# Two-operand elementwise work from GpSimd to VectorE, first expert loads before the gather, LN2's first results in PSUM

## The chip, the cores and the metric

The kernel runs on one core of one Trainium2 chip, in one launch. The metric is device time in microseconds, the median of the runs shown; smaller is better. Five engines take part, each with a queue of its own: TensorE (PE, with its weight loads as PEld), VectorE (DVE), ScalarE (ACT), GpSimd (POOL), and SyncE (SP), which issues most DMAs.

## The reference

A sequence of 256 tokens with 1024 features goes through two blocks, all in float32. The first block is two hybrid layers and a norm; the second is one mixer with four branches, LayerNorm (LN1), a mixture of experts and LayerNorm again (LN2). Cut to what matters:

```
# hybrid_layer, twice
h = rms_norm(x, norm_mix_g) * (1 + sc_m) + sh_m
proj = h @ w_in
...
merged = (jax.nn.sigmoid(ga) * (o_na @ w_br_na)
          + jax.nn.sigmoid(gb) * (o_mla @ w_br_mla)
          + jax.nn.sigmoid(gc) * (o_gqa @ w_br_gqa))
x = x + g_m * (merged @ w_out)
h = rms_norm(x, norm_ffn_g) * (1 + sc_f) + sh_f
gate, up = jnp.split(h @ ffn_w_gate_up, 2, axis=-1)
x = x + g_f * ((jax.nn.silu(gate) * up) @ ffn_w_down)
# second_block
h = mixer(x, ...)
x = layer_norm(DN_ALPHA * x + h, ln1_g[l], ln1_b[l])
h = moe(x, w_router, router_bias, w_gate[l], w_up[l], w_down[l])
x = layer_norm(DN_ALPHA * x + h, ln2_g[l], ln2_b[l])
```

Each token goes to 2 of 16 experts. The kernel collects each expert's tokens by matrix products with a selection matrix P (the gather); an expert is two 1024x512 products, an activation, and one 512x1024 product.

## The kernel before

**Matrix products in three.** Every float32 matrix is split into a high part (rounded to fp32r) and a low remainder, and a product is three matmuls: high x high (line 189), and the two mixed ones (190 and 191). For weights, `raw` lets SP load up to 1 MB (128 x 2048, line 152) into a ring of buffers (`wr`); `pieces` makes each half of it, 128 x 1024, into two parts: ACT casts the high part (`wh`, line 159), and DVE subtracts (`wl`, line 164), or POOL does (line 162). The rings `wh` and `wl` have five buffers each. For activations, ACT casts (231, 276, 306) and DVE subtracts (232, 277, 307).

**Who subtracts.** `s.hold` is a list that `pieces` takes one entry from: POOL, or an instruction behind which the subtraction must stand, or nothing. `norm_end` fills it with three entries of POOL from the table `HOLD`, so the first three weight pieces loaded after it are subtracted by POOL. `moe` fills it for the first expert: two pieces by DVE, two by POOL, two by DVE behind the building of P.

```
a = s.hold.pop(0) if s.hold else None
if a is s.nc.gpsimd:
    a.tensor_sub(lo, src, hi)
```

**Other POOL work with two operands.** The squares that a norm sums up over four pairs of feature blocks: POOL adds the second and third, DVE the fourth (`norm_add`, 288). The gated sum of the three branches, two adds for each of four column blocks and each layer (816, 16 in all). The mask of the neighbourhood attention (695, 8), the last add of the rotary step (538, 6), the gated merge of the mixer's branches (1544, 8), one quarter of LN1's second token half (1716 and 1717, behind an ACT step at 1715), the low parts of LN1's output (1728 and 1827), and the last quarter of LN2 (1983 and 1984). POOL also issues DMAs: the modulation weights (400), the attention bias (690) and constants.

**Order.** The program is written in stage order, and a scheduler then orders each engine's queue by the data that each instruction needs; a queue is worked off in its order. So the place of an instruction in a queue isn't always that of the code. Names in the rows begin with a stage: `L_lat`, `L_gqaqkv` and others are the head of a layer (its projections), `L_branch` and `L_wout` the end of its attention, `L_gu` and `L_down` its FFN; `M_` is the mixer (`M_rg` and `M_gdn` its first branches, `M_out` its output projection, `M_ln` LN1), `E_` the experts.

**LN1 to the gather** (`out_norm`, `route`, `moe`). The output projection is computed in eight tiles; behind the tiles of a token half stand the statistics, the normalised rows `x2` (`norm_apply`, two DVE steps of 128 x 256 for each quarter, 1642 and 1643), the router's score, the selection, the slot numbers `pos`, the matrix P (1841), then the gather's products (1852), which ACT and DVE copy out of PSUM (1855, 1857). The gather is a generator: it yields after each product.

**The end** (`out_rows`). LN2's sums stand in four PSUM banks of 128 x 512, `z`. For three of them `norm_apply` reads PSUM and writes to SBUF (1642), then reads that and writes the output rows (1643); the fourth goes over ACT and POOL. Each is stored by its own DMA (1987).

## Time and profile before

| | |
|---|---|
| runs | 1613.37 us median of 3 (1607.16 to 1614.84) |
| the profiled execution | 1609.31 us, of which the profile's span is 1607.5 |
| PE, DVE, ACT, POOL busy in the span | 96%, 75%, 56%, 14% |
| granted clock of PE, mean over the span | 0.985 of full speed |
| DMA, mean over the span | 215 GB/s |

The profile is of one execution, whose own time is in the second line. Busy shares are over the whole span; where an engine waits, the view of waits names the engine and line that it waited for, and the timeline lists instructions with start, duration and, in brackets, the idle time before one. A duration in the timeline that carries x2 or x4 is of that many instructions in a row together.

### The profile page before, as it was taken

To read this page: it belongs to the slowest core of one execution; us is meant where nothing else is said; L and a number is where in the kernel's file an instruction comes from. 1 tells how busy PE (TensorE), PEld (TensorE's weight loads), DVE (VectorE), ACT (ScalarE), POOL (GpSimd) and SP (SyncE) were. 2 spreads that over 40 slices of the span, in tenths; PEclk is the share of its full clock that TensorE was granted. 3 is DMA by queue.
4 is the path that set the end of the run, shared out by engine and by line. 5 is a ranking of instruction groups with operands and counts; after the bars stand their busy time and mean duration, and the time that the engine had idled before them with its cause. 6 is when DMAs were issued, how large, how long until landed. Compare 5 with 4: busy or idle time off the path is not lost.

```text
span 1607.5 us, 28047 instructions
## 1 busy us (share of the span) xinstructions
PE 1541.4 (96%) x11376; PEld 1419.1 (88%) x11376; DVE 1208.0 (75%) x1615; ACT 900.9 (56%) x1316; POOL 218.7 (14%) x236
## 2 busy tenths in 40 slices
PE   7899999999999999899998999999999899999996
PEld 5789999999987989899998989999999778888884
DVE  5889778767597886784547976567666788988886
ACT  4555546444465554544445771665565377777774
POOL 0221033102032102400002004112020110000000
PEclk9999999999999999999999999999999899999998
DMA  9678547886556864665553650334556489999982
GB/s 349 220 251 282 165 151 256 293 281 213 169 170 215 285 208 139 212 233 184 184 186 124 185 158 27 106 105 138 179 180 213 139 321 333 333 325 334 340 324 94
DMA packets 206055, 345.77 MB, mean 215 GB/s; under 512 B 6928, under 2 KB 175008, under 8 KB 193632
## 3 DMA queue, kind: packets, MB, share of 16 engines
q1 hardware_dynamic: 191040, 294.42, 54.9%
q0 software_dynamic: 12512, 45.64, 7.9%
q10 hardware_dynamic: 2368, 3.86, 0.7%
q8 instruction: 91, 1.49, 0.4%
q14 instruction: 44, 0.36, 0.1%
HBM read 342.84 MB, written 1.05 MB: 214 GB/s over the span
## 4 chain that ended last, share of the span: by engine, by line
PE 85%; DVE 8%; ACT 3%; POOL 2%; issue 1%; DMA 1%; DVEq 0%; POOLq 0%; ACTq 0%
PE L_gu.mm L190 5%; PE L_gu.mm L191 4%; PE L_gu.mm L189 4%; PE L_att.mm L189 3%; PE L_att.mm L191 3%; PE L_att.mm L190 3%; PE M_merge.mm L191 2%; PE M_merge.mm L189 2%; PE M_merge.mm L190 2%; PE E_gu.mm L189 2%; PE E_gu.mm L191 2%; PE E_gu.mm L190 2%; PE L_gu.s L190 1%; PE L_gu.s L189 1%; PE L_gu.s L191 1%; PE L_att.s L424 1%
## 5 line engine op out<-in xcount | busy, mean ns | idle before, releaser
L190 PE MATMUL L_gu.mm<-L_fnorm.hl,L_gu.wh 128*128 128x256 f32 x640 | 178.9, 280 | 0.2
L191 PE MATMUL L_gu.mm<-L_fnorm.hh,L_gu.wl 128*128 128x256 f32 x640 | 178.9, 280 | 0.0
L189 PE MATMUL L_gu.mm<-L_fnorm.hh,L_gu.wh 128*128 128x256 f32 x640 | 178.6, 280 | 0.1
L164 DVE TENSOR_TENSOR E_gu.wl<-E_gu.wr,E_gu.wh 128x1024 fp32r<-128x1024 f32 x126 | 153.7, 1241 | 19.6 <-ACT E_gu.wh L159 16.3
L159 ACT CAST L_gu.wh<-L_gu.wr 128x1024 fp32r<-128x1024 f32 x84 | 88.2, 1050 | 119.7 <-PE L_gu.mm L190 79.2
L159 ACT CAST E_gu.wh<-E_gu.wr 128x1024 fp32r<-128x1024 f32 x128 | 132.8, 1054 | 36.7 <-PE E_gu.mm L191 10.2
L164 DVE TENSOR_TENSOR L_gu.wl<-L_gu.wr,L_gu.wh 128x1024 fp32r<-128x1024 f32 x78 | 96.3, 1238 | 66.3 <-ACT L_gu.wh L159 66.1
L189 PEld LDWEIGHTS L_gu.mm<-L_fnorm.hh,L_gu.wh 128*128 128x128 f32 x640 | 120.2, 188 | 0.5 <-ACT L_fnorm.hh L306 0.5
L190 PEld LDWEIGHTS L_gu.mm<-L_fnorm.hl,L_gu.wh 128*128 128x128 f32 x640 | 120.1, 188 | 0.6 <-DVE L_fnorm.hl L307 0.6
L191 PEld LDWEIGHTS L_gu.mm<-L_fnorm.hh,L_gu.wl 128*128 128x128 f32 x640 | 120.3, 188 | 0.0
L159 ACT CAST L_down.wh<-L_down.wr 128x1024 fp32r<-128x1024 f32 x48 | 50.5, 1051 | 77.0 <-PE L_gu.mm L190 42.9
L393 DVE SCALAR_TENSOR_TENSOR ada.big<-ada.big,sc,ada.big 128x1024 f32<-128x1024 f32 x70 | 92.3, 1318 | 0.2
L164 DVE TENSOR_TENSOR L_down.wl<-L_down.wr,L_down.wh 128x1024 fp32r<-128x1024 f32 x48 | 59.8, 1246 | 40.2 <-ACT L_down.wh L159 40.1
L164 DVE TENSOR_TENSOR E_down.wl<-E_down.wr,E_down.wh 128x1024 fp32r<-128x1024 f32 x64 | 75.5, 1222 | 4.3 <-ACT E_down.wh L159 4.2
L159 ACT CAST L_att.wh<-L_att.wr 128x1024 fp32r<-128x1024 f32 x44 | 46.2, 1051 | 55.4 <-PE L_att.mm L190 48.3
L400 POOL DMA_DIRECT2D ada.big<-in_ada_w x80 | 42.4, 532 | 251.4 <-DVE ada.big L393 160.4
L164 DVE TENSOR_TENSOR M_merge.wl<-M_merge.wr,M_merge.wh 128x1024 fp32r<-128x1024 f32 (+1 forms) x50 | 55.2, 1109 | 27.8 <-ACT M_merge.wh L159 27.8
L159 ACT CAST E_down.wh<-E_down.wr 128x1024 fp32r<-128x1024 f32 x64 | 65.8, 1057 | 13.0 <-PE E_down.mm L191 4.5
L159 ACT CAST M_merge.wh<-M_merge.wr 128x1024 fp32r<-128x1024 f32 (+1 forms) x50 | 41.9, 843 | 43.8 <-PE M_merge.mm L190 40.2
L191 PE MATMUL M_merge.mm<-fnorm.hh,M_merge.wl 128*128 128x256 f32 x208 | 59.1, 284 | 0.0
L189 PE MATMUL M_merge.mm<-fnorm.hh,M_merge.wh 128*128 128x256 f32 x208 | 58.0, 279 | 0.0
L190 PE MATMUL M_merge.mm<-fnorm.hl,M_merge.wh 128*128 128x256 f32 x208 | 57.8, 278 | 0.0
(972 smaller groups left out, 5552.5 us busy)
## 6 DMA issues: line engine op xcount, KB each, us to landing
...
```

Source lines behind the costliest of these rows:

```text
L159: s.nc.scalar.copy(hi, src)
L164: i = s.nc.vector.tensor_sub(lo, src, hi).ins
L189: mm(ps, ah, bh, start=first and fresh and k == 0, stop=False, skip_group_check=True)
L190: mm(ps, ah, bl, start=False, stop=False, skip_group_check=True)
L191: mm(ps, al, bh, start=False, stop=last and k == n - 1, skip_group_check=True)
L393: nc.vector.scalar_tensor_tensor(acc, raw, c, acc, op0=ALU.mult, op1=ALU.add)
L400: s.tc.keep_in_program_order(nc.gpsimd.dma_start(raw, s.I["ada_w"][l, k * 128:(k + 1) * 128, v * 1024:(v + 1) * 1024]))
L424: nc.tensor.matmul(S[e][:, b], q[e][:, b * 128:(b + 1) * 128], k[e], start=True, stop=True)
```

## The change

All of the two-operand work named above except LN2's last quarter goes from POOL to DVE, and the table `HOLD` goes. LN1's quarter goes through `norm_apply` like the others. The low part of LN1's first token half stands behind the next tile in the code, that of the second half behind the building of P. The first expert's gate weights are loaded and cast ahead of the gather (`early`): the first load with its subtractions, the second with its subtractions collected in `s.defer` and issued after the gather's steps. The first gather takes all high parts before the low parts. LN2's first step writes its result back into PSUM, and the second step reads it from there.

```diff
@@ -17,7 +17,6 @@
 NB = 6
-HOLD = [3, 3, 3, 3]
@@ -109,6 +108,7 @@
         s.more, s.nraw = None, 0
+        s.defer = None
@@ -158,12 +158,12 @@
         a = s.hold.pop(0) if s.hold else None
-        if a is s.nc.gpsimd:
-            a.tensor_sub(lo, src, hi)
-        else:
-            i = s.nc.vector.tensor_sub(lo, src, hi).ins
-            if a:
-                s.after(i, a)
+        if s.defer is not None:
+            s.defer.append(lambda: s.nc.vector.tensor_sub(lo, src, hi))
+            return hi, lo
+        i = s.nc.vector.tensor_sub(lo, src, hi).ins
+        if a:
+            s.after(i, a)
@@ -285,11 +285,9 @@
         else:
-            (nc.vector if i == 3 else nc.gpsimd).tensor_add(s.zq, s.zq, q)
+            nc.vector.tensor_add(s.zq, s.zq, q)
...
     def norm_end(s, **k):
-        s.hold = [s.nc.gpsimd] * HOLD[0]
-        HOLD.append(HOLD.pop(0))
@@ -535,7 +533,7 @@
         nc.vector.scalar_tensor_tensor(qn[:, :nj], qn[:, :nj], f, bc(C["cg"]), op0=ALU.mult, op1=ALU.mult)
-        nc.gpsimd.tensor_add(qg[:, 2 * i:2 * i + nj], qn[:, :nj], sb[:, :nj])
+        nc.vector.tensor_add(qg[:, 2 * i:2 * i + nj], qn[:, :nj], sb[:, :nj])
@@ -692,7 +690,7 @@
                 bv = b.rearrange("p (d c) -> p d c", c=64)
-                nc.gpsimd.tensor_tensor(bv, bv, C["mask"].unsqueeze(1).to_broadcast([128, 8, 64]), ALU.add)
+                nc.vector.tensor_tensor(bv, bv, C["mask"].unsqueeze(1).to_broadcast([128, 8, 64]), ALU.add)
@@ -813,7 +811,7 @@
                     t2 = s.t([128, 512], "b2", NB)
-                    nc.gpsimd.tensor_add(t2, m, t)
+                    nc.vector.tensor_add(t2, m, t)
@@ -1541,7 +1539,7 @@
             if not first:
-                (nc.vector if out else nc.gpsimd).tensor_add(mi, mi, t)
+                nc.vector.tensor_add(mi, mi, t)
@@ -1710,13 +1708,7 @@
                         c = slice(q * 256, (q + 1) * 256)
-                        if b and q == 3:
-                            v = x2[:, b, c]
-                            nc.scalar.activation(v, ax[b][:, c], AF.Identity, bias=mr[:, b:b + 1], scale=r[:, b:b + 1])
-                            nc.gpsimd.tensor_mul(v, v, g[:, c])
-                            nc.gpsimd.tensor_add(v, v, bb[:, c])
-                        else:
-                            s.norm_apply(x2, ax[b][:, c], mv, r, g, bb, b, c)
+                        s.norm_apply(x2, ax[b][:, c], mv, r, g, bb, b, c)
@@ -1725,7 +1717,8 @@
                 nc.scalar.copy(xh[:, 0], x2[:, 0])
-                nc.gpsimd.tensor_sub(xl[:, 0], x2[:, 0], xh[:, 0])
+            if (i, b) == (2, 1):
+                nc.vector.tensor_sub(xl[:, 0], x2[:, 0], xh[:, 0])
@@ -1824,7 +1817,6 @@
         s.after(nc.scalar.copy(xh[:, 1], x2[:, 1]).ins, s.load_ins)
-        nc.gpsimd.tensor_sub(xl[:, 1], x2[:, 1], xh[:, 1])
@@ -1840,22 +1832,24 @@
                                             s.C3["iota"].unsqueeze(1).to_broadcast([128, 2, SLOTS]), ALU.is_equal).ins
+            G[g] = P, gh, gl
+            todo = [(k, src, dst) for k in range(0, 8, 2) for src, dst in ((xh, gh), (xl, gl))]
             if g == 0:
-                s.hold = [None, None, nc.gpsimd, nc.gpsimd, i, i]
-            G[g] = P, gh, gl
-            for k in range(0, 8, 2):
-                for src, dst in ((xh, gh), (xl, gl)):
-                    LAB[0] = 'E_gather.'
-                    p = bank()
-                    for i in range(2):
-                        for b in range(2):
-                            nc.tensor.matmul(p[:, i * 256:(i + 1) * 256], src[:, b, (k + i) * 128:(k + i + 1) * 128], P[:, b], start=b == 0, stop=b == 1)
-                    d = f(dst[:, k:k + 2])
-                    if src is xh:
-                        nc.scalar.copy(d, p)
-                    else:
-                        nc.vector.tensor_copy(d, p)
-                    yield
+                s.after(nc.vector.tensor_sub(xl[:, 1], x2[:, 1], xh[:, 1]).ins, i)
+                todo = todo[::2] + todo[1::2]
+                yield
+            for k, src, dst in todo:
+                LAB[0] = 'E_gather.'
+                p = bank()
+                for i in range(2):
+                    for b in range(2):
+                        nc.tensor.matmul(p[:, i * 256:(i + 1) * 256], src[:, b, (k + i) * 128:(k + i + 1) * 128], P[:, b], start=b == 0, stop=b == 1)
+                d = f(dst[:, k:k + 2])
+                if src is xh:
+                    nc.scalar.copy(d, p)
+                else:
+                    nc.vector.tensor_copy(d, p)
+                yield
@@ -1875,13 +1869,15 @@
+        early = []
+
...
             for c in range(2):
-                w = s.load_mov(I[W][e, c], 4, 512)
+                w = early.pop(0) if early else s.load_mov(I[W][e, c], 4, 512)
@@ -1918,9 +1914,13 @@
         G = {}
-        s.more = s.a
+        early.append(s.load_mov(I["wg"][0, 0], 4, 512))
...
         next(steps)
+        s.defer = []
+        early.append(s.load_mov(I["wg"][0, 1], 4, 512))
+        later, s.defer = s.defer, None
+        s.more = s.a
@@ -1933,6 +1933,8 @@
             pass
+        for sub in later:
+            sub()
@@ -1977,13 +1979,15 @@
                 c = slice(d * 512, d * 512 + 512)
+                v = o[:, b, c]
                 if b * d:
-                    v = o[:, b, c]
...
                 else:
-                    s.norm_apply(o, z[b][d], mv, r, g, bb, b, c)
+
+                    nc.vector.scalar_tensor_tensor(z[b][d], z[b][d], mv[:, b, 0:1], g[:, c], op0=ALU.subtract, op1=ALU.mult)
+                    nc.vector.scalar_tensor_tensor(v, z[b][d], r[:, b:b + 1], bb[:, c], op0=ALU.mult, op1=ALU.add)
```

Line numbers of the changed kernel differ by a few from those before. The order of DVE's queue is shown at three places, from the built programs. First, ahead of the FFN of layer 0; `L_wout.hl` is the low part of the scaled residual that `L_gu` multiplies, `L_wout.b` the sum of squares. Before:

```order
L832 SCALAR_TENSOR_TENSOR x_86<-L_wout.mm_2688,L_wout.gm_2534,x_86 128x256 x2
L277 SCALAR_TENSOR_TENSOR L_wout.hl_2540<-x_86,L_wout.gm_2536,L_wout.hh_2539 128x256 x2
L832 SCALAR_TENSOR_TENSOR x_86<-L_wout.mm_2766,L_wout.gm_2534,x_86 128x256 x2
L277 SCALAR_TENSOR_TENSOR L_wout.hl_2540<-x_86,L_wout.gm_2536,L_wout.hh_2539 128x256 x2
L288 TENSOR_TENSOR L_wout.b_2604<-L_wout.b_2604,L_wout.b_2817 128x512
L164 TENSOR_TENSOR L_gu.wl_3014<-L_gu.wr_3007,L_gu.wh_3013 128x1024
```

and with the change:

```order
L830 SCALAR_TENSOR_TENSOR x_86<-L_wout.mm_2688,L_wout.gm_2534,x_86 128x256 x2
L164 TENSOR_TENSOR L_gu.wl_2930<-L_gu.wr_2927,L_gu.wh_2929 128x1024
L277 SCALAR_TENSOR_TENSOR L_wout.hl_2540<-x_86,L_wout.gm_2536,L_wout.hh_2539 128x256 x2
L288 TENSOR_TENSOR L_wout.b_2604<-L_wout.b_2604,L_wout.b_2739 128x512
L164 TENSOR_TENSOR L_gu.wl_2934<-L_gu.wr_2927,L_gu.wh_2933 128x1024
L830 SCALAR_TENSOR_TENSOR x_86<-L_wout.mm_2766,L_wout.gm_2534,x_86 128x256 x2
L164 TENSOR_TENSOR L_gu.wl_3010<-L_gu.wr_3007,L_gu.wh_3009 128x1024
L277 SCALAR_TENSOR_TENSOR L_wout.hl_2540<-x_86,L_wout.gm_2536,L_wout.hh_2539 128x256 x2
L288 TENSOR_TENSOR L_wout.b_2604<-L_wout.b_2604,L_wout.b_2817 128x512
L164 TENSOR_TENSOR L_gu.wl_3014<-L_gu.wr_3007,L_gu.wh_3013 128x1024
```

POOL's three weight subtractions and two norm adds now stand in DVE's queue, one subtraction right ahead of the last two splits (277).

Second, from layer 1 to the mixer; `L_down.hl` is the same split for the mixer's first products, `fnorm` the norm that ends block one. Before:

```order
L277 SCALAR_TENSOR_TENSOR L_down.hl_9585<-x_86,L_down.gm_9582,L_down.hh_9584 128x256 x4
L288 TENSOR_TENSOR L_down.b_9606<-L_down.b_9606,L_down.b_9682 128x512
L246 TENSOR_TENSOR fnorm.b_9696<-fnorm.wl_9690 128x256
L247 SCALAR_TENSOR_TENSOR fnorm.b_9696<-fnorm.o_9691,fnorm.b_9696 128x256
L248 SCALAR_TENSOR_TENSOR fnorm.wl_9690<-fnorm.b_9696,fnorm.wl_9690 128x256
L1022 SCALAR_TENSOR_TENSOR x_86<-x_86,L_down.gm_9582,fnorm.wl_9690 128x256 x4
L232 TENSOR_TENSOR fnorm.hl_9701<-x_86,fnorm.hh_9700 128x256 x4
L1022 SCALAR_TENSOR_TENSOR x_86<-x_86,L_down.gm_9582,fnorm.wl_9690 128x256 x3
```

and with the change:

```order
L277 SCALAR_TENSOR_TENSOR L_down.hl_9585<-x_86,L_down.gm_9582,L_down.hh_9584 128x256 x2
L288 TENSOR_TENSOR L_down.b_9606<-L_down.b_9606,L_down.b_9661 128x512
L862 SCALAR_TENSOR_TENSOR x_86<-L_gu.t_7720,mod_91,x_86 128x256
L277 SCALAR_TENSOR_TENSOR L_down.hl_9585<-x_86,L_down.gm_9582,L_down.hh_9584 128x256 x2
L288 TENSOR_TENSOR L_down.b_9606<-L_down.b_9606,L_down.b_9682 128x512
L164 TENSOR_TENSOR M_rg.wl_9834<-M_rg.wr_9831,M_rg.wh_9833 128x1024
L246 TENSOR_TENSOR fnorm.b_9696<-fnorm.wl_9690 128x256
L164 TENSOR_TENSOR M_rg.wl_9838<-M_rg.wr_9831,M_rg.wh_9837 128x1024
L247 SCALAR_TENSOR_TENSOR fnorm.b_9696<-fnorm.o_9691,fnorm.b_9696 128x256
L164 TENSOR_TENSOR M_gdn.wl_9941<-M_gdn.wr_9938,M_gdn.wh_9940 128x1024
L248 SCALAR_TENSOR_TENSOR fnorm.wl_9690<-fnorm.b_9696,fnorm.wl_9690 128x256
L164 TENSOR_TENSOR M_gdn.wl_9978<-M_gdn.wr_9975,M_gdn.wh_9977 128x1024
```

The four splits now stand in pairs among the norm adds, and four weight subtractions stand ahead of and among the steps of the norm (246 to 248); POOL had three of them, and one stood further down.

Third, behind the last but one tile of LN1; `E_gather.wl` are the first expert's low parts (162 is a deferred subtraction), `M_out.hl` the low part of LN1's output. Before:

```order
L1694 SCALAR_TENSOR_TENSOR M_out.b_13820<-M_out.mm_14104,M_out.b_13820 128x256
L164 TENSOR_TENSOR E_gu.wl_14317<-E_gu.wr_14310,E_gu.wh_14316 128x1024
L1694 SCALAR_TENSOR_TENSOR M_out.b_13820<-M_out.mm_14130,M_out.b_13820 128x256
L1699 BN_STATS M_out.lnst_13855<-M_out.b_13820 128x6
L1633 BN_AGGR M_out.lnmv_13856<-M_out.lnst_13855 128x2
```

and with the change:

```order
L1692 SCALAR_TENSOR_TENSOR M_out.b_13820<-M_out.mm_14103,M_out.b_13820 128x256
L164 TENSOR_TENSOR E_gather.wl_14236<-E_gather.wr_14229,E_gather.wh_14235 128x1024
L1721 TENSOR_TENSOR M_out.hl_13854<-M_out.x_13852,M_out.hh_13853 128x1024
L1692 SCALAR_TENSOR_TENSOR M_out.b_13820<-M_out.mm_14130,M_out.b_13820 128x256
L162 TENSOR_TENSOR E_gather.wl_14248<-E_gather.wr_14245,E_gather.wh_14247 128x1024
L1697 BN_STATS M_out.lnst_13855<-M_out.b_13820 128x6
L1757 SCALAR_TENSOR_TENSOR M_out.b_13858<-M_out.o_13851,lnr,M_out.b_13858 128x16
L1631 BN_AGGR M_out.lnmv_13856<-M_out.lnst_13855 128x2
L162 TENSOR_TENSOR E_gather.wl_14251<-E_gather.wr_14245,E_gather.wh_14250 128x1024
L1707 SCALAR_TENSOR_TENSOR M_out.lnmr_13857<-M_out.lnmv_13856,lnr 128x1
```

The deferred subtractions of line 162 stand among the statistics of the second token half, and not behind the gather, where the code issues them.

## Rows read from the trace of the kernel before

**Rows 1.** The page, parts 1 and 4: busy time of each engine, chain by engine.

```profile
PE 1541.4 (96%) x11376; PEld 1419.1 (88%) x11376; DVE 1208.0 (75%) x1615; ACT 900.9 (56%) x1316; POOL 218.7 (14%) x236
...
PE 85%; DVE 8%; ACT 3%; POOL 2%; issue 1%; DMA 1%; DVEq 0%; POOLq 0%; ACTq 0%
```

**Rows 2.** Who waited for whom, PE alone: us in total, times, longest us.

```profile
PE M_rg.mm L190 <- DVE L_down.hl L277: 4.4, 3, 1.9
PE L_wout.mm L189 <- ACT L_branch.hh L231: 4.0, 2, 2.0
PE L_gu.s L190 <- DVE L_wout.hl L277: 3.7, 2, 1.9
...
PE L_lat.mm L190 <- DVE L_lat.hl L307: 3.3, 3, 1.8
PE L_gu.t L189 <- DVE x L864: 3.2, 1, 3.2
PE E_route.o L1795 <- DVE sel L1792: 3.1, 1, 3.1
PE E_gu.o L190 <- POOL E_gu.wl L162: 2.0, 2, 1.6
```

**Rows 3.** Timeline at the router: start us, us, engine, line, operation, out<-in, count.

```profile
1274.09 2.34 POOL L1827 TENSOR_TENSOR M_out.hl<-M_out.x,M_out.hh 128x1024 fp32r<-128x1024 f32 x1 [3.12 <-ACT M_out.hh L1826]
1274.16 2.32 DVE L1778 TENSOR_TENSOR E_route.b<-E_route.b,cst 128x32 f32<-128x32 f32 x1
```

**Rows 4.** Timeline before layer 0's FFN.

```profile
251.50 5.09 POOL L162 TENSOR_TENSOR L_gu.wl<-L_gu.wr,L_gu.wh 128x1024 fp32r<-128x1024 f32 x2
...
252.31 0.88 DVE L832 SCALAR_TENSOR_TENSOR x<-L_wout.mm,L_wout.gm,x 128x256 f32<-128x256 f32 x2 [0.47 <-PE L_wout.mm L191]
...
253.72 3.15 DVE L277 SCALAR_TENSOR_TENSOR L_wout.hl<-x,L_wout.gm,L_wout.hh 128x256 fp32r<-128x256 f32 x2 [0.54 <-ACT L_wout.hh L276]
```

**Rows 5.** Timeline from layer 0's branches to its output projection.

```profile
227.06 0.68 DVE L811 SCALAR_TENSOR_TENSOR L_branch.b<-L_att.big,L_branch.s 128x512 f32<-128x512 f32 x1
...
227.65 1.22 DVE L164 TENSOR_TENSOR L_wout.wl<-L_wout.wr,L_wout.wh 128x1024 fp32r<-128x1024 f32 x1
...
227.88 4.43 POOL L816 TENSOR_TENSOR L_branch.b<-L_branch.b,L_branch.b 128x512 f32<-128x512 f32 x2 [2.12 <-DVE L_branch.b L811]
...
228.79 0.68 DVE L811 SCALAR_TENSOR_TENSOR L_branch.b<-L_att.big,L_branch.t 128x512 f32<-128x512 f32 x1
...
232.35 0.62 ACT L231 CAST L_branch.hh<-L_branch.b 128x512 fp32r<-128x512 f32 x1 [3.92 <-POOL L_branch.b L816]
```

**Rows 6.** Groups by line and shape, POOL: largest and smallest of the 17 that move.

```profile
L816 POOL TENSOR_TENSOR L_branch.b<-L_branch.b,L_branch.b 128x512 f32<-128x512 f32 x16 | 29.3, 1831 | 92.2 <-DVE L_branch.b L811 91.9
...
L1717 POOL TENSOR_TENSOR M_out.x<-M_out.x,M_out.b 128x256 f32<-128x256 f32 x1 | 0.8, 785 | 0.1
```

**Rows 7.** Timeline, DVE, layer 0's first projections.

```profile
56.80 2.89 DVE L307 SCALAR_TENSOR_TENSOR L_lat.hl<-L_gqaqkv.nt,mod,L_lat.hh 128x256 fp32r<-128x256 f32 x2
```

**Rows 8.** Timeline, DVE, end of layer 0's FFN.

```profile
443.63 1.98 DVE L277 SCALAR_TENSOR_TENSOR L_down.hl<-x,L_down.gm,L_down.hh 128x256 fp32r<-128x256 f32 x1
...
445.93 2.58 DVE L277 SCALAR_TENSOR_TENSOR L_down.hl<-x,L_down.gm,L_down.hh 128x256 fp32r<-128x256 f32 x1
```

**Rows 9.** Stretches: engines' busy us (x instructions), granted clock, DMA share, GB/s.

```profile
450.00:460.00 10.00, 10.00 (x69) 9.89 (x69) 8.23 (x13) 6.66 (x12) 5.82 (x3) 0.83 0.32 103
```

**Rows 10.** Timeline, end of layer 1 and start of the mixer.

```profile
860.53 7.19 DVE L277 SCALAR_TENSOR_TENSOR L_down.hl<-x,L_down.gm,L_down.hh 128x256 fp32r<-128x256 f32 x4
...
882.28 0.36 PE L189 MATMUL M_gdn.mm<-L_down.hh,M_gdn.wh 128*128 128x256 f32 x1 [1.67 <-DVE M_rg.b L1486]
```

**Rows 11.** Timeline, DVE, the end of the program.

```profile
1594.12 0.73 DVE L1642 SCALAR_TENSOR_TENSOR E_end.out<-M_ln.s,E_end.ln2mv,E_gather.lng 128x512 f32<-128x512 f32 x1
...
1595.59 2.41 DVE L1643 SCALAR_TENSOR_TENSOR E_end.out<-E_end.out,E_end.ln2r,E_gather.lnb 128x512 f32<-128x512 f32 x2
```

**Rows 12.** Stretches, the experts (columns as in rows 9).

```profile
1300.00:1560.00 260.00, 260.00 (x1214) 213.60 (x1213) 230.90 (x236) 199.10 (x223) 0.00 (x0) 1.00 0.92 334
```

## The prediction

> **What bounds the kernel now.** I read the page's busy times and its chain first. TensorE (PE) is busy for 96% of the span and makes up 85% of the chain that ended last; VectorE (DVE) makes up 8% of the chain and GpSimd (POOL) 2% [rows 1]. So a microsecond counts only where PE stands still. Next comes the view of who waited for whom, for PE alone. Seven of its lines have a DVE instruction or POOL's result behind them in a place that the change touches; they add up to 4.4 + 4.0 + 3.7 + 3.3 + 3.2 + 3.1 + 2.0 = 23.7 us [rows 2]. POOL itself is named only in the last one. Then I went to the timelines at these seven places and looked at what DVE was doing while POOL ran.
>
> **What the timelines show.** A DVE instruction with two operands in SBUF becomes long while a POOL two-operand instruction runs. The clearest case: a 128x32 operation of the router took 2.32 us from 1274.16, beside a POOL subtraction from 1274.09 that took 2.34 [rows 3]; both ended at about 1276.4. Two normalisation splits of 128x256 took 3.15 us beside POOL [rows 4], where two 128x256 steps take 0.88 in the same view. POOL is long too: two adds of 128x512 took 4.43 us [rows 5]. The seven waits are mostly this.
>
> **Prices.** Unstretched, a 128x512 step of DVE costs 0.59 us (from 227.06 to 227.65) and a 128x1024 subtraction 1.14 (from 227.65 to 228.79) [rows 5]; a 128x256 step costs 0.44 (half of 0.88) [rows 4]. The change takes 17 groups off POOL, from 29.3 us down to 0.8 [rows 6], 64 instructions and 117 us in all, and one ScalarE (ACT) step. DVE gets 16 x 1.14 + 44 x 0.59 + 4 x 0.44 = 46 us more. Against that stands the refund on stretched instructions, so I expect its busy time to end near where it is, and POOL's at about 100 us. Neither is the answer: each place has to be replayed in its new order, because the moved instructions now stand in DVE's queue, often ahead of the one that PE waits for.
>
> **The sum, place by place** (gains in us; the replay starts from the traced start times and puts the prices above into the new order).
>
> - *Layer 0 head.* The pair of splits at 56.80 took 2.89 instead of 0.88 [rows 7], 2.0 too long. One mask add (0.59) moves ahead of them and three more (1.8) ahead of the next weight subtraction, which PE needs soon after. I take 1.2; ends 0 and 3.3, the whole wait.
> - *Branches to the output projection, two layers.* POOL's two adds end at 232.3, and ACT's cast starts at 232.35 [rows 5]. On DVE the second add would end at about 230.8: the products come first, with two weight subtractions between. So the high half is 1.5 earlier; the low half has one more subtraction ahead of it and is 1.2 earlier. 1.2 x 2 = 2.4. Ends 0.6 x 2 = 1.2 (if the third product comes no earlier than today) and 4.0.
> - *Norm before the FFN, two layers.* The awaited pair at 253.72 loses 2.3 to POOL. In the new order one weight subtraction stands right ahead of it, but ACT's cast for that one is done when DVE gets there. 1.6 x 2 = 3.2; ends 1.0 and 3.7.
> - *Layer 0 to layer 1.* Two splits took 1.98 and 2.58 [rows 8] instead of 0.44: 3.7 lost, of which PE waits 3.2. Four mask adds and two norm adds now stand among them, and a weight subtraction ahead of the eighth split. 2.2; ends 0 and 4.9: PE's granted clock is 0.83 in the 10 us behind this wait [rows 9], between its levels 2.4 and 1.2 GHz, and 1.7 us of that would come back at most.
> - *Layer 1 head.* Little contention, but three rotary adds and a subtraction enter DVE's chain: -0.5; ends -2 and 0.
> - *Layer 1 to the mixer.* Four splits took 7.19 [rows 10] instead of 1.7. That is the largest refund, and most of it is given back: the place ends where PE waits for DVE's product at 882.28 [rows 10], and in front of that product the new order has three more weight subtractions (3.4) and two norm adds (1.2) among the splits. 5.5 - 3.4 - 1.2 = 0.9; ends 0 and 4.4.
> - *LayerNorm, route, gather.* The router gets back 2.1 [rows 3] and PE's 2.0 of waiting for POOL's expert weights goes. But the order places both "deferred" subtractions not behind the gather: they stand among the LayerNorm's statistics, a third one sits between two router instructions, and the split of the first token half is there too. Three of these fall behind the last output tile: the router starts 3.4 later (3 x 1.14), its selection 3.4 - 2.1 = 1.3 later. 2.0 - 1.3 = 0.7; ends -1.5 and 4.1, both refunds.
> - *End.* Two LN2 steps took 2.41 [rows 11]; unstretched they would take 1.3. The trace has no LN2 step from PSUM to PSUM. I bound it by 0.59 and by twice that, and take it near the low end, since the step from PSUM to SBUF in the same place took 0.73 [rows 11]. The last store moves by 0.8; ends -1.0 (three steps at twice the price, 1.8 more) and 1.2.
>
> The rest of the moved work lies beside PE: the eight merge adds have no PE wait behind them, and from 1300 to 1560 PE is busy 260 of 260 us [rows 12] with POOL idle, so this stretch neither gains nor loses and only starts earlier. The early expert loads cost SP nothing: it issues the same DMAs, the second one moved from fifth place to second; the casts wait for weight buffers that PE's last output tiles free, which is in the router's term. POOL's own loads are passed by fewer instructions.
>
> Sum: 1.2 + 2.4 + 3.2 + 2.2 - 0.5 + 0.9 + 0.7 + 0.8 = 10.9 us. The profiled execution took 1609.31 us (span 1607.5), so it would take 1598.4; that execution lies 4.1 below the median of the three runs, 1613.37, so the median becomes **1602.5 us**.
>
> **A rule on the last term.** The Trainium skill ("VectorE: DVE Perf Modes", Specifications) says that VectorE sits closer to SBUF and ScalarE closer to PSUM; by it the three results kept in PSUM would be dearer, not cheaper. No run here shows that yet. The Trainium skill's "Perfetto Trace Analysis" (Optimizing Scalar/DVE Operations) has an overhead of about 60 ns for SBUF and 125 for PSUM, so by it the last term would be 0.2 smaller, as an estimate; the sum doesn't use it.
>
> **Rivals.**
> 1. *Everything is given back* (chance 0.16). DVE has one queue, and the instruction that stretched another now stands ahead of it: three subtractions of 1.14 cost 3.4, the refund of two splits is 2.3 to 3.6. With all low ends the sum is 0 + 1.2 + 1.0 + 0 - 2 + 0 - 1.5 - 1.0 = -2.3, so the time would be 1613 to 1616. For it: the layer 1 to mixer place, replayed above. Against it: the norm before the FFN, where a single subtraction stands ahead. The Trainium skill says the same in "Perfetto Trace Analysis" (Optimizing Scalar/DVE Operations): since the two engines share a read port, moving work between them might not help. By it the time would be that of this rival; the trace agrees about the contention [rows 3] and not yet about the outcome.
> 2. *All of it comes back* (0.17). If DVE reaches the awaited instructions ahead of PE everywhere, the seven waits go: 23.7 + 0.8 = 24.5, or 1589. For it: DVE is idle for a quarter of the span [rows 1]. Against it: in the replays it is just the heads where it isn't.
> 3. *Slower: the length isn't POOL's doing* (0.07). If the long splits come from something else, say transfers, nothing is refunded, and DVE is late by the moved steps wherever PE waits for it. That is all that moves but the eight merge adds: 46 - 8 x 0.59 = 41. DVE's idle time there takes up perhaps half, 20; the waits on POOL's results that go take off 4.0 + 2.0. 20 - 6 = 14: 1627. It decides from the point where a lone 128x256 split still takes over about 1.5 us, halfway between 0.44 [rows 4] and 2.58 [rows 8], with POOL idle. Against it: the common end at 1276.4.
>
> **How the numbers follow.** The forecast's own range is 4 to 18 us of gain (1595 to 1609), chance 0.60. A measurement of this kernel tells about 0.5% from no change, 8 us. Three quarters of the forecast lie beyond that (0.45), with rival 2's 0.17 that makes 0.62 for faster; a quarter of it (0.15) and rival 1 make 0.31 for no change; rival 3 is 0.07. The range 1590 to 1613 holds the forecast, rival 1's upper side and half of rival 2.
>
> **What would show it.** Right: POOL's busy time at about 100 us, DVE's within 20 us of 1208; no 128x256 split above 0.6 us beside the norms; PE's waits for the splits before the FFN under 0.5 us each; the wait for the product in front of M_gdn still there; no wait for POOL's expert weights; the selection later against the last output tile than today. Wrong: splits still over 1.5 us (rival 3), or PE's waits the same length with another name behind them (rival 1). If the sum is right in total but the last two places gained, the replay of the router was wrong.

## The result and the profile after

The changed kernel takes 1591.62 us, the median of 4 runs (1588.89 to 1593.63), beside 1614.11 for 4 runs of the kernel before: a ratio of 0.9879, interval 0.9857 to 0.9902. It is faster by 1.2%; the forecast was 1602.5 (0.7%), the range 1590 to 1613. In the profiled executions the span went from 1607.5 to 1588.5 us, 18.9 less where the sum had 10.9.

The page, parts 1 and 4 (busy time of each engine; the chain by engine), against [rows 1]:

```profile
PE 1534.7 (97%) x11376; PEld 1413.4 (89%) x11376; DVE 1199.7 (76%) x1679; ACT 904.2 (57%) x1315; POOL 101.5 (6%) x172
...
PE 68%; issue 23%; DVE 4%; ACT 2%; DMA 2%; POOL 0%; ACTq 0%; DVEq 0%; POOLq 0%; SPq 0%
```

POOL lost 117 us and DVE none, though it runs 64 instructions more: the refund on stretched instructions pays for all of them. The chain's 23% of "issue" are no waits of PE: 307 us of it, from 1270.52, are POOL's idle queue ahead of its last quarter of LN2, over which the chain is followed back, and 47 us lie at the start. Up to the gather the two chains can be compared: DVE's part there went from about 117 us to 58. The view of who waited for whom, PE alone (us in total, times, longest), against [rows 2]:

```profile
PE L_gqaqkv.mm L189 <- ACT L_naqkv.big L730: 6.6, 2, 5.1
PE M_gdn.mm L189 <- DVE M_rg.b L1484: 3.8, 1, 3.8
PE M_gdn.ad L189 <- ACT M_gdn.wh L159: 2.0, 1, 2.0
PE E_route.o L1788 <- DVE sel L1785: 1.7, 1, 1.7
...
PE L_lat.mm L190 <- DVE L_lat.hl L305: 1.2, 2, 0.7
...
PE M_rg.mm L190 <- DVE L_down.hl L277: 0.4, 1, 0.4
```

Of the seven waits, those before the output projection, before the FFN, for the residual and for POOL's expert weights are gone, and three are shorter. Other waits are long now: 6.6 in the layers' heads (5.1 in layer 0, 1.5 in layer 1), 3.8 before M_gdn (1.67 at [rows 10]) and, just ahead of that one, a new one of 2.0 for a weight that ACT casts.

**Where it was gained.** PE runs 11,376 matmuls in every kernel here, so the start of its n-th matmul can be laid side by side, and the lead that a kernel gains from one n to another is the gain of that place. In us, from one profiled execution each (before minus kernel; e1 to e10 are the experiments of the next section):

| place (n) | forecast | after | e1 | e2 | e3 | e10 |
|---|---|---|---|---|---|---|
| start, layer 0 head (0 to 800) | 1.2 | 0.6 | 0.2 | -2.9 | 0.5 | 0.5 |
| branches, layer 0 (1600 to 1800) | 1.2 | 2.66 | 2.66 | 0 | -1.51 | 0 |
| norm before FFN, layer 0 (1800 to 2000) | 1.6 | 2.56 | 0.01 | 1.58 | 2.55 | 0.02 |
| layer 0 to 1 (3200 to 3600) | 2.2 | 0.73 | 0.01 | 2.48 | -0.07 | -3.03 |
| layer 1 head (3600 to 4000) | -0.5 | 2.30 | 1.45 | 1.31 | 2.34 | 1.37 |
| branches, layer 1 (4800 to 5100) | 1.2 | 4.20 | 4.21 | 1.53 | 1.65 | 0.38 |
| norm before FFN, layer 1 (5100 to 5300) | 1.6 | 2.58 | 0 | 2.58 | 2.59 | 0 |
| layer 1 to mixer (6400 to 7200) | 0.9 | 0.92 | -0.96 | 1.27 | 1.50 | -1.17 |
| LayerNorm, route, gather (9600 to 10000) | 0.7 | 1.89 | -0.49 | -0.17 | 1.88 | 1.50 |
| end (last matmul to span) | 0.8 | 0.61 | 0 | 0 | 0.32 | 0.61 |
| span | 10.9 | 18.9 | 6.9 | 7.5 | 11.8 | 0.3 |

Two cautions. The start moves by 3 us from execution to execution (it waits for the first loads), and "layer 0 to 1" reads -3.03 in e10, which has the order of before there: in e10 a norm add of DVE waited for POOL, and PE waited 1.8 us for it (the rows are in the last section). Also, 1.3 to 1.7 us in layer 1's head and at its branches appear in kernels that changed nothing at that place. PE's granted clock goes with them, as the stretches show (busy us of PE, PEld, DVE, ACT, POOL with instructions, granted clock, DMA share, GB/s), first before:

```profile
495.00:505.00 10.00, 9.74 (x60) 8.16 (x60) 5.72 (x10) 3.44 (x7) 3.25 (x5) 0.83 0.69 211
640.00:650.00 10.00, 7.68 (x58) 7.28 (x57) 5.43 (x7) 4.28 (x7) 4.34 (x2) 0.93 0.42 138
```

The same work after, 6 to 9 us earlier:

```profile
490.00:500.00 10.00, 9.98 (x84) 9.72 (x84) 5.81 (x11) 4.08 (x7) 4.67 (x10) 1.00 0.90 267
630.00:640.00 10.00, 10.00 (x85) 9.88 (x85) 8.21 (x14) 5.03 (x7) 0.87 (x2) 1.00 0.95 302
```

And the branches of layer 1 in e2, which leaves them as they were:

```profile
640.00:650.00 10.00, 7.67 (x63) 7.27 (x62) 6.54 (x11) 4.32 (x9) 7.64 (x9) 1.00 0.78 266
```

Before, PE had stood for 1.9 us (until 494.71) ahead of the first of these stretches and 2.0 for the branches in the second; the clocks of 0.83 and 0.93 (0.90 in the next 10 us) are means between its levels, 2.4 and 1.2 GHz. After, the wait at the branches is gone and the one in the head is 1.5 us, and the clock is full. But the wait alone doesn't decide it: at layer 1's branches PE stands the same 2.0 us in e2 and e3, and in its head 2.4 to 2.5 in two waits in e1, e2 and e10, with a clock of 1.00 behind. So of the 18.9 us some 1.4 in the head and 1.5 at the branches is the clock of the execution of before, and it isn't shown that the change wins it. Over whole runs the clock is higher where the time is lower: 0.993 to 0.994 in the five runs of e11 (the fastest version, below), 0.982 to 0.988 in the nine of the kernel before beside them.

### The profile page after: what moved, and what is told of

Its sections match the earlier page's. It is cut to its first block, busy times and chain, and to the rows that moved or that the text cites. A ratio compares the mean times of both kernels' runs of the same rounds, so it can differ in the third digit from the quotient of the medians.

```text
span 1588.5 us, 27970 instructions
## 1 busy us (share of the span) xinstructions
PE 1534.7 (97%) x11376; PEld 1413.4 (89%) x11376; DVE 1199.7 (76%) x1679; ACT 904.2 (57%) x1315; POOL 101.5 (6%) x172
## 4 chain that ended last, share of the span: by engine, by line
PE 68%; issue 23%; DVE 4%; ACT 2%; DMA 2%; POOL 0%; ACTq 0%; DVEq 0%; POOLq 0%; SPq 0%
PE L_gu.mm L189 5%; PE L_gu.mm L191 5%; PE L_gu.mm L190 5%; PE L_att.mm L189 3%; PE L_att.mm L191 3%; PE L_att.mm L190 3%; PE M_merge.mm L191 2%; PE M_merge.mm L189 2%; PE M_merge.mm L190 2%; PE L_gu.s L189 2%; PE L_gu.s L190 2%; PE L_gu.s L191 1%; PE L_gu.t L191 1%; PE L_gu.t L190 1%; PE L_gu.t L189 1%
## 5 line engine op out<-in xcount | busy, mean ns | idle before, releaser
L164 DVE TENSOR_TENSOR E_gu.wl<-E_gu.wr,E_gu.wh 128x1024 fp32r<-128x1024 f32 x124 | 150.1, 1224 | 21.3 <-ACT E_gu.wh L159 17.0
L164 DVE TENSOR_TENSOR L_gu.wl<-L_gu.wr,L_gu.wh 128x1024 fp32r<-128x1024 f32 x84 | 102.7, 1225 | 71.0 <-ACT L_gu.wh L159 70.3
L164 DVE TENSOR_TENSOR M_merge.wl<-M_merge.wr,M_merge.wh 128x1024 fp32r<-128x1024 f32 (+1 forms) x50 | 48.2, 969 | 30.5 <-ACT M_merge.wh L159 30.5
```

The lines of the kernel that those rows point to most:

```text
L164: i = s.nc.vector.tensor_sub(lo, src, hi).ins
```

## The experiments

The theory: DVE's and POOL's two-operand instructions keep each other from running, so every wait of [rows 2] is partly POOL's work beside DVE's, and each goes with the instructions that cause it. The rivals: the gain is from the parts of the change that move no work (early loads, the gather's order, PSUM), or from one place alone. Each ratio below is against runs of the kernel before on the same chip.

**e1: the kernel before, with the branch adds on DVE.**

```diff
-                    nc.gpsimd.tensor_add(t2, m, t)
+                    nc.vector.tensor_add(t2, m, t)
```

> The kernel before with one edit: the 16 adds of the gated branch sum (line 816) on VectorE, all other GpSimd work left. Theory (GpSimd's two-operand work is late itself and lengthens VectorE's instructions, all the way up the chain of products and adds): both waits of about 2.1 and 0.6 us at the output projection go in each layer, the first output-projection product comes about 2.7 us earlier in layer 0, and in layer 1 another 2.7 and about 1.4 from the granted clock; the total is 6 to 7 us lower, 0.996 of before. The waits of 2.0 us before the FFN stay. Forecast of the replay: 1.2 per layer, 2.4 in all. Rival (the gain of the change comes from the new order of the weight subtractions, not from GpSimd): under 0.5 here.

1603.71 us (median of 10), ratio 0.9951 (0.9926 to 0.9976). At the branches it gains 2.66 and 4.21, what the whole change gains there to 0.01 us, and nothing at the norm. Some 1.5 of the 4.21 is the clock, which e2 and e3 gain there without this line. The other 2.7 a layer is explained by this one line, and my 1.2 a layer was too little.

**e2: the kernel before, with the norm work on DVE** (the adds of squares, and the three weight subtractions behind each norm).

```diff
-            (nc.vector if i == 3 else nc.gpsimd).tensor_add(s.zq, s.zq, q)
+            nc.vector.tensor_add(s.zq, s.zq, q)
...
-        s.hold = [s.nc.gpsimd] * HOLD[0]
-        HOLD.append(HOLD.pop(0))
```

> The kernel before with the norms' work alone moved: the three weight subtractions behind each norm and the two norm adds (288) on VectorE; the branch adds stay on GpSimd. Theory: the wait for the splits before the FFN (2.0 us per layer) goes and 2.5 us come back in each layer, the places between the layers and before the mixer give 1 to 4 more; the total is 6 to 9 us lower, the waits of 2.1 at the output projection stay. Forecast of the replay: 1.6 per layer before the FFN, 0 to 2 at each place behind it, 4 to 6 in all. Rival (the subtractions in VectorE's queue give it all back): within 1 us.

1599.94 (median of 8), ratio 0.9921 (0.9887 to 0.9956). PE's waits in e2:

```profile
PE L_wout.mm L189 <- ACT L_branch.hh L231: 4.0, 2, 2.0
PE M_gdn.mm L189 <- DVE M_rg.b L1484: 3.8, 1, 3.8
...
PE L_gu.s L190 <- DVE L_wout.hl L277: 0.5, 1, 0.5
```

Of the wait before the FFN 0.5 is left, and that for the branches stands whole: the two are independent. The longer wait of 3.8 before M_gdn comes with this part of the change. The norm gains 1.58 and 2.58 (after: 2.56 and 2.58). Most of layer 0's other 1.0 is the 0.5 in the last line and 0.2 just ahead of it: both lie in layer 0, where in e2 a weight subtraction (255.28 to 256.50) stands in front of the residual's last two steps.

**e3: the change, with the branch adds back on POOL** (the line of e1 reversed).

> The changed kernel with the 16 branch adds back on GpSimd. Theory: the waits at the output projection come back, 2.7 us in layer 0 and 2.7 to 4.1 in layer 1, so 5 to 7 us slower than the changed kernel. Forecast of the replay: 2.4 slower. Rival (order): no difference.

1598.08 (median of 7), ratio 0.9917 (0.9887 to 0.9947). The 4.0 us wait is back, and the branches lose 4.17 and 2.55 against the change. The waits are the same in both layers, 2.0 for the high part and 0.3 for the low; in layer 1 the clock behind them is 1.00, and in layer 0 the stretch (columns as above) shows it lower:

```profile
230.00:240.00 10.00, 7.62 (x50) 7.22 (x50) 5.39 (x8) 4.97 (x7) 5.55 (x8) 0.83 0.97 349
```

**e4: the change, with the three subtractions behind each norm back on POOL** (`HOLD` and its use in `pieces` and `norm_end` as before).

```diff
+        if a is s.nc.gpsimd:
+            a.tensor_sub(lo, src, hi)
+            return hi, lo
...
+        s.hold = [s.nc.gpsimd] * HOLD[0]
+        HOLD.append(HOLD.pop(0))
```

> The changed kernel with the three weight subtractions behind each norm back on GpSimd, the norm adds left on VectorE. Theory: the splits before the FFN are over 1.5 us a pair again, beside GpSimd, and 2 to 4 us are lost over the two layers, with 0 to 3 more between the layers and before the mixer; 2 to 6 us slower than the changed kernel. Rival (the subtractions in VectorE's queue cost as much as they give back): -3 to +1.

1600.65 (median of 10), ratio 0.9929 (0.9906 to 0.9952): 0.5% behind the change by the ratios, more than expected. In the profile 2.26 a layer are lost at the norm, 3.5 between the layers, 1.9 in the head. The timeline of e4 before layer 0's FFN (start us, us, engine, line, operation, out<-in):

```profile
249.19 2.56 POOL L166 TENSOR_TENSOR L_gu.wl<-L_gu.wr,L_gu.wh 128x1024 fp32r<-128x1024 f32 x1 [0.37 <-ACT L_gu.wh L160]
249.42 2.88 DVE L292 TENSOR_TENSOR L_wout.b<-L_wout.b,L_wout.b 128x512 f32<-128x512 f32 x1
```

DVE's add, 0.68 when alone, ends at 252.30 since POOL ran until 251.75. A norm add moved to DVE is no help while the subtractions stay on POOL: it then waits for them itself, in front of the split.

**e5 and e6: the change, with three idle POOL instructions beside each norm**, two-operand adds in e5, copies in e6, that nothing reads. They tell whether two operands on POOL are needed to block DVE.

```diff
+            if i:
+                nc.gpsimd.tensor_add(s.t([128, 512], "dum", 1).rearrange("p (a b) -> p a b", a=2), x[:, 2 * i:2 * i + 2], x[:, 2 * i:2 * i + 2])
```

> The changed kernel with three GpSimd adds of 128x512 beside the splits of each of the four norms, reading the same blocks twice and writing a tile that nothing reads; no result changes and no instruction of VectorE moves. Theory (a GpSimd instruction with two operands in SBUF lengthens VectorE's): the pairs of splits (277), 0.88 us alone, take 1.8 to 3.2 beside the adds, TensorE waits 0.5 to 2 us for the last pair before each FFN, and 2 to 8 us are lost in all. Rival (the length isn't GpSimd's doing, only late inputs or order): the pairs stay at 0.88 and the first FFN matmuls come at the same time.

> The same three GpSimd instructions at the same places, but copies (one operand read). Theory in its strict form (two operands are what lengthens): the pairs of splits stay below 1.0 us and nothing is lost. If any GpSimd work that reads and writes SBUF lengthens VectorE's: 1.3 us or more a pair, as with the adds.

1596.32 and 1597.88, one execution each. The timeline of e5 before layer 0's FFN, and POOL's add where DVE runs nothing beside it (848.92):

```profile
251.31 1.23 DVE L164 TENSOR_TENSOR L_gu.wl<-L_gu.wr,L_gu.wh 128x1024 fp32r<-128x1024 f32 x1
251.32 2.11 POOL L290 TENSOR_TENSOR L_wout.dum<-x 128x512 f32<-128x512 f32 x1 [3.54 <-DVE x L832]
252.45 1.66 DVE L277 SCALAR_TENSOR_TENSOR L_wout.hl<-x,L_wout.gm,L_wout.hh 128x256 fp32r<-128x256 f32 x2
...
848.92 1.15 POOL L290 TENSOR_TENSOR L_down.dum<-x 128x512 f32<-128x512 f32 x1 [1.24 <-DVE x L864]
```

The pair of splits is a little under the 1.8 expected, and the norm loses 0.8 us a layer against the change. DVE's subtraction began 0.01 us ahead and keeps its 1.23. POOL's add takes 2.11 instead of 1.15, and then the splits behind it take 1.66 instead of 0.87. So it isn't that both run at half speed: one runs and the other waits, each in turn. The same in e6:

```profile
253.10 1.22 DVE L164 TENSOR_TENSOR L_gu.wl<-L_gu.wr,L_gu.wh 128x1024 fp32r<-128x1024 f32 x1
253.10 1.70 POOL L290 COPY L_wout.dum<-x 128x512 f32<-128x512 f32 x1 [3.95 <-DVE x L832]
254.24 1.23 DVE L277 SCALAR_TENSOR_TENSOR L_wout.hl<-x,L_wout.gm,L_wout.hh 128x256 fp32r<-128x256 f32 x2
...
850.13 0.74 POOL L290 COPY L_down.dum<-x 128x512 f32<-128x512 f32 x1 [1.66 <-DVE x L864]
```

The norm loses 0.3 a layer. A copy blocks too, for the shorter time that it takes (0.74 alone; the pair takes 1.23, just under the 1.3 expected, and not 0.87), so my strict form of the theory, two operands on both sides, falls. On DVE's side it matters where the operands are: the steps of LN2 that read one from PSUM were not blocked (the rows are at "the end" below). The Trainium skill ("SBUF — State Buffer", SBUF: two separate sides) calls the port pair that the two engines share an exclusive lock: whoever starts first holds it for a whole instruction and the other blocks. The trace agrees, with the 1.23 against the 2.11 above; which of two starts first isn't always to be seen (last section).

**e7: the change, with the mask adds put behind the next weight subtractions.** It is aimed at the wait that the change lengthened, 5.1 in layer 0's head. Its chain in the profile after:

```profile
58.97 1.89 DVE L693 TENSOR_TENSOR L_nab.big<-L_nab.big,cst 128x512 f32<-128x512 f32 x3
60.78 1.22 DVE L164 TENSOR_TENSOR L_gqaqkv.wl<-ada0.wr,L_gqaqkv.wh 128x1024 fp32r<-128x1024 f32 x1
...
67.29 0.37 SPq L152 DMA_DIRECT2D L_mlaup.wr<-in_w_uq  x1
...
74.67 1.05 ACT L159 CAST L_mlaup.wh<-L_mlaup.wr 128x1024 fp32r<-128x1024 f32 x1 [4.38 <-DMA L_mlaup.wr<-in_w_uq]
...
76.25 0.58 PE L189 MATMUL L_gqaqkv.mm<-L_lat.hh,L_gqaqkv.wh 128*128 128x256 f32 x1 [5.08 <-ACT L_naqkv.big L730]
```

Three mask adds stand ahead of a weight subtraction. The subtractions free buffers of the ring, so a load starts late, ACT's cast waits for it 4.38 us, and behind that cast in ACT's queue stands the copy out of PSUM that PE waits for.

```diff
         w = s.load_mov(w_in[:, 512:768], 8, 256)
+        for b in bias:
+            bv = b.rearrange("p (d c) -> p d c", c=64)
+            s.after(nc.vector.tensor_tensor(bv, bv, C["mask"].unsqueeze(1).to_broadcast([128, 8, 64]), ALU.add).ins, s.sub)
```

> The changed kernel with the eight mask adds (693) put behind the last weight subtraction of the neighbourhood projections, in both layers. Theory (a moved step costs where it stands ahead of the awaited one in VectorE's queue): the wait of 5.24 us at 76 us, for a weight whose load waits for a buffer that a late subtraction frees, shrinks to 1 to 3 us, the waits of 0.7 and 1.3 at 457 to 460 go, and 1 to 5 us are won against the changed kernel. Rival (the masks lie beside other work): within 1 us of it.

1585.36 (median of 4), ratio 0.9826 (0.9773 to 0.9879), 5.4 below the change in the profile. The load is issued at 63.89 and not at 67.29 and is no longer waited for; ACT's cast follows PE:

```profile
71.32 1.04 ACT L159 CAST L_mlaup.wh<-L_mlaup.wr 128x1024 fp32r<-128x1024 f32 x1 [1.49 <-PE L_naqkv.mm L190]
```

Against the change the head, counted from the first matmul, gains 2.75 and the passage between the layers 1.75. That is under the 3 us by which the start moves, but behind the start the order decides: from the 400th to the 800th matmul the kernels with the masks in the change's place (the change, e3, e8, e12) lose 1.2 to 2.4 against before, and those with the masks late (e7, e9, e11) gain 1.6. So the moved mask adds cost about 2.8 there, and nearly the whole of the 3.3 that I had given as that term's upper end was to be had.

**e8: the change, with the first expert's subtractions kept behind the selection.**

```diff
-            sub()
+            s.after(sub(), s.pins)
+        s.hold = [s.pins] * 2
```

> The changed kernel with the second load's two weight subtractions and the third load's first two forced behind the building of P. Theory (my step that three of these in front of the selection cost 3 x 1.14): the selection comes 2 to 3 us earlier after the last output tile, and the first expert's products start 1.5 to 3 us earlier. Rival (given back): VectorE is then behind in the first expert, PE waits there for subtractions, and the gain by the 2000th matmul of the experts is under 0.5 us.

1587.67 (median of 4), ratio 0.9848 (0.979 to 0.9907). The stretch from the last output tile to the selection, DVE's timeline after:

```profile
1250.17 0.42 DVE L1692 SCALAR_TENSOR_TENSOR M_out.b<-M_out.mm,M_out.b 128x256 f32<-128x256 f32 x1
1250.50 1.22 DVE L162 TENSOR_TENSOR E_gather.wl<-E_gather.wr,E_gather.wh 128x1024 fp32r<-128x1024 f32 x1
...
1253.12 1.17 DVE L162 TENSOR_TENSOR E_gather.wl<-E_gather.wr,E_gather.wh 128x1024 fp32r<-128x1024 f32 x1
...
1257.82 1.22 DVE L164 TENSOR_TENSOR E_gu.wl<-E_gu.wr,E_gu.wh 128x1024 fp32r<-128x1024 f32 x1
...
1261.86 0.19 DVE L1785 SCALAR_TENSOR_TENSOR sel<-E_route.b 128x32 bf16<-128x32 f32 x1
```

and in e8:

```profile
1251.46 0.42 DVE L1692 SCALAR_TENSOR_TENSOR M_out.b<-M_out.mm,M_out.b 128x256 f32<-128x256 f32 x1
...
1260.06 0.19 DVE L1785 SCALAR_TENSOR_TENSOR sel<-E_route.b 128x32 bf16<-128x32 f32 x1
```

11.7 us become 8.6, and the 3.0 gained here are kept to the end: the three subtractions that the replay saw in this stretch are its cost.

**e9, e11 and e12: all three heads reordered.** e9 is e7 and e8 together, and in the mixer only the first two rows of the final norm stand ahead of the product that M_gdn waits for; for that the gain is copied into a tile of its own, since its place is used again.

```diff
+        xf, g = x, s.t([128, 8], "gz", 1, pool=s.xp)
+        nc.vector.tensor_copy(g, s.zg)
...
+                if k > 1:
+                    s.after(i, s.prod)
```

> The changed kernel with three places reordered and no work left out: the mask adds behind the neighbourhood weights, four expert subtractions behind the selection, and six of the final norm's eight steps (1020) behind the mixer's two products (1484), for which TensorE waited 3.8 us behind weight subtractions and the norm's steps. Theory: the gains of the two separate runs add up (5.4 and 3.0 us), and 1 to 4 us come from the product; 9 to 12 us faster than the changed kernel, 1578 to 1583. If the final norm's late steps are then waited for instead, the place gives -2 to +1 and the total is 7 to 9.

1584.35 (median of 5), ratio 0.9838 (0.9819 to 0.9856): 5.9 in the profile against the change, not the 9 to 12. The places, the head again from the first matmul, gained 3.7, 1.7, 1.0 (the product) and 3.0, but 3.1 was lost evenly over the experts and 1.7 in the two FFNs, where nothing was edited, and 1.2 won within the mixer. The new tile of 128 x 8 moves what is allocated behind it by 32 bytes in each partition. e11 keeps the order and puts the gain in free columns of a tile that exists:

```diff
-        xf, g = x, s.t([128, 8], "gz", 1, pool=s.xp)
+        r = s.t([128, 1024], "wl", WH, pool=s.w)
+        g, r = r[:, 256:264], r[:, :256]
```

e12 is the change with an unused tile of that size and nothing else:

```diff
+        nc.vector.memset(s.t([128, 8], "gz", 1, pool=s.xp), 0.0)
```

> The kernel with three places reordered, but the copy of the norm's gain (128x8) stands in free columns of a tile that is there anyway, so that no tile in SBUF is moved by 32 bytes. Theory (the 3 us that the reordered kernel lost evenly over the experts, 512-column products at 233 ns in place of 230, came from the moved addresses): 230 ns again, nothing lost between the first expert's product and the last, 8 to 10 us faster than the changed kernel by the trace, 1580 to 1583. Rival (it came from the new order): the loss of about 3 us over the experts stays.

> The changed kernel with nothing but an unused tile of 128x8 in the pool of the norms' results, which moves every tile behind it by 32 bytes per partition, and one memset at the start. Theory of the addresses: 512-column products of the experts at 233 ns, 2 to 4 us lost between the first and the last expert. Rival: at 230, under 0.5 us.

e11 takes 1580.25 (median of 5, 1578.91 to 1580.76), ratio 0.9801 (0.9784 to 0.9818): **the fastest version, 2.0% below the kernel before**, and 10.0 us below the change in the profile (3.4, 1.8, 1.1, 3.0 at the four places and 0.3 at the experts). e12 took 1602.63 in one execution; its total isn't read, since its granted clock dips (0.91 in the stretch 170 to 190, where the change has 1.00), but its rows at full clock are. The group of one of three matmuls of the experts, from 1290 to 1560 us (count, busy us, mean ns), after:

```profile
L190 PE MATMUL E_gu.mm<-E_gu.wl,E_gu.xgh 128*128 128x512 f32 x96 | 37.4, 390 | 0.0
```

in e12, with the unused tile alone:

```profile
L190 PE MATMUL E_gu.mm<-E_gu.wl,E_gu.xgh 128*128 128x512 f32 x81 | 32.0, 395 | 0.0
```

e9, with the new tile, has 395 too, and e11 390 again; the clock is 1.00 in this stretch in all four. From the 10,000th to the 11,300th matmul the change takes 279.7 us, e11 279.5, e9 282.8 and e12 283.0.

**e10: the change, with all moved work back on POOL** but the first expert's subtractions. What is left of the change is the early loads, the gather's order and LN2 in PSUM.

> The changed kernel with every two-operand step back on GpSimd but the first expert's subtractions; what is left of the change is the early loads of the first expert, the order of the gather and LN2's results in PSUM. Theory: nothing changes before the selection, TensorE's 2.0 us of waiting for the expert weights goes, the end gives 0.5 to 0.8; 1 to 3 us faster than before, and the selection is late as before beside GpSimd. Rival (these parts carry the gain): 5 us or more.

1607.86 (median of 10), ratio 0.9984 (0.9968 to 0.9999). The parts that move no work gain at most 2.1 us in the profile, 1.5 at the gather and 0.6 at the end, and PE's waits are those of [rows 2] again, but for that for POOL's expert weights, which is gone, and the router's, which is 4.2 under another name (LN1's rows):

```profile
PE L_wout.mm L193 <- ACT L_branch.hh L235: 4.0, 2, 2.0
...
PE L_gqaqkv.s L536 <- DVE L_gqaqkv.b L527: 3.7, 3, 1.3
...
PE L_norm.o L244 <- DVE L_down.b L292: 1.8, 1, 1.8
```

The last line is new; it goes with the -3.03 between the layers. So the move itself makes nearly all of the gain.

## Why the prediction was right, and which terms were not

**The total.** The mechanism held and the size didn't: the sum was 10.9 us and the span fell by 18.9. The measured 1591.62 lies below the forecast's own 1595 to 1609 and is inside 1590 to 1613 only because that range took in half of rival 2. Some 3 us of the excess are the clock of the execution of before; the rest is in the terms below.

**What held.** The reading of the bound (microseconds count only where PE stands), the cause (POOL's work beside DVE's), the prices (a 128x512 add on DVE 0.69 in the rows after, 0.59 net), and every sign of "what would show it": POOL at 101.5, DVE within 9 us of 1208, a split before the FFN at 0.44 (half of 0.87), no wait there, the M_gdn wait still there (longer, 3.8), no wait for POOL's expert weights, the selection 11.7 us behind the last output tile instead of 10.7.

**The branches: 2.4 forecast, 6.9 gained.** The step that failed is the replay's start: it took the products at their traced times. The timeline after:

```profile
226.48 0.68 DVE L809 SCALAR_TENSOR_TENSOR L_branch.b<-L_att.big,L_branch.t 128x512 f32<-128x512 f32 x1
...
227.46 1.22 DVE L164 TENSOR_TENSOR L_wout.wl<-L_wout.wr,L_wout.wh 128x1024 fp32r<-128x1024 f32 x1
228.60 0.69 DVE L814 TENSOR_TENSOR L_branch.b<-L_branch.b,L_branch.b 128x512 f32<-128x512 f32 x1
...
229.31 0.62 ACT L231 CAST L_branch.hh<-L_branch.b 128x512 fp32r<-128x512 f32 x1 [1.98 <-DVE L_branch.b L814]
```

The kernel is 0.6 ahead here already, so the third product stands at 227.07 on the clock of before, not 228.79 [rows 5]. That it was late in before is itself POOL's doing: in e1, where only the adds moved, it starts at 226.87. One weight subtraction lies between the product and its add, not two, and the cast starts 3.0 earlier (2.4 net). That and the low part's wait of 0.3 make the 2.7 a layer. The rest, some 1.5 in layer 1, is granted clock, which e2 and e3 have there with the wait of 2.0 in place: it isn't shown to come from the move.

**The norm before the FFN: 3.2 forecast, 5.1 gained.** The timeline after:

```profile
250.06 1.22 DVE L164 TENSOR_TENSOR L_gu.wl<-L_gu.wr,L_gu.wh 128x1024 fp32r<-128x1024 f32 x1
251.20 0.87 DVE L277 SCALAR_TENSOR_TENSOR L_wout.hl<-x,L_wout.gm,L_wout.hh 128x256 fp32r<-128x256 f32 x2
```

The one weight subtraction stands ahead of the pair, as said, and the pair is at its bare 0.87. The kernel is 3.25 ahead here, so on the clock of before the pair ends 1.55 earlier, as replayed. But the whole wait of 1.9 went, not 1.6: I replayed DVE alone, while PE's queue also changed its order and puts four more products (0.5 us) in front of the one that needs the pair's second split. Of the other 0.7 a layer, 0.3 lies right at the wait and 0.4, in layer 0, at three matmuls about the 1950th, where before is slower; their cause was not looked for.

**Layer 1's head: -0.5 forecast, +2.3 gained.** The sign was wrong. 1.3 to 1.5 of it is clock: e1, e2 and e10 have it too, with the wait for the rotary chain (L523 before) still at 3.7 us and the clock at 1.00 in 495 to 505 of e10. Most of the other 0.9 goes with that chain, whose wait I left out of the seven, though before has it:

```profile
PE L_gqaqkv.s L532 <- DVE L_gqaqkv.b L523: 3.4, 3, 1.9
```

In layer 1 it was 1.9 and 0.3, and it is gone there, with 1.5 for ACT's copy (L730) in its place. I saw little contention there and charged the adds that enter DVE's chain; what they refund is more.

**LayerNorm, route, gather: 0.7 forecast, 1.9 gained.** By e10, 1.5 of it comes without any moved two-operand work but the first expert's. Whether that is the wait of 2.0 for POOL's expert weights, which the forecast had counted and which is gone in e10, or the order of gather and loads, which I had costed at nothing, no run separates; in e10 the selection stands 12.5 us behind the last output tile. The replay of the router was right: three subtractions in front of the selection, and e8 gets 3.0 back by taking them out.

**Head, 1.2 against 0.6; layer 0 to 1, 2.2 against 0.7.** The first is less than the 3 us by which starts differ. The second isn't chance: with the masks in the change's place the passage reads -0.3 to 0.8 (the change, e3, e8, e12), with the masks late 2.47 to 2.49 (e7, e9, e11). So what the low values hold is the mask adds, which I had let take back 2.1 in the head: they delay a weight buffer, and through a load, a cast and a copy make one wait of 5.1. I followed the subtraction and not the load behind it.

**Layer 1 to mixer, 0.9 against 0.92.** Refund and price were both seen: the waits for the splits fell from 4.4 to 0.4, and the two before M_gdn rose from 1.7 to 5.8. That the difference agrees to 0.02 is luck: kernels with the same order there read 1.50 (e3), 1.18 (e8) and -0.19 (e12).

**The end, 0.8 against 0.6**, held. e10 has the 0.6 without moved work, so it is the PSUM result itself. Its rows after:

```profile
1575.79 0.74 DVE L1989 SCALAR_TENSOR_TENSOR M_ln.s<-M_ln.s,E_end.ln2mv,E_gather.lng 128x512 f32<-128x512 f32 x1
...
1577.26 1.40 DVE L1990 SCALAR_TENSOR_TENSOR E_end.out<-M_ln.s,E_end.ln2r,E_gather.lnb 128x512 f32<-128x512 f32 x2
```

A step from PSUM to PSUM took 0.74, that from PSUM to SBUF before 0.73 [rows 11]. The Trainium skill's "VectorE: DVE Perf Modes" (Specifications) says that VectorE sits closer to SBUF, by which PSUM would be the dearer place; the rows don't show it. What the change wins here is a step that POOL doesn't block: POOL still works on its quarter (1.26 us from 1577.58), and the second steps, which now read PSUM, take 1.40 beside it. Before, two of them, reading SBUF alone, took 2.41 beside POOL [rows 11], while a first step, which reads PSUM, was not stretched:

```profile
1597.53 1.59 POOL L1984 TENSOR_TENSOR E_end.out<-E_end.out,E_gather.lnb 128x512 f32<-128x512 f32 x1
1597.92 0.74 DVE L1642 SCALAR_TENSOR_TENSOR E_end.out<-M_ln.t,E_end.ln2mv,E_gather.lng 128x512 f32<-128x512 f32 x1
```

**The rivals.** Rival 1, everything given back, falls: 18.9 of the 24.5 came, some 16 without the clock. The Trainium skill ("Perfetto Trace Analysis", Optimizing Scalar/DVE Operations) says that moving work between these engines might not help, as they share a port. Here it does help. A reason that the rows offer, not tested by itself, is that the same 128x512 add blocks the other engine for 1.15 us on POOL and takes 0.69 on DVE. Rival 3 falls with the split at 0.44. Rival 2, all of it, is within reach once the moved work stands behind the awaited instructions: e11's span is 29.0 us below that of before, over the 24.5, which left out the clock and waits not among the seven.
